# Attention stage of a hybrid decoder trunk: all score tiles scaled right behind the softmax's join, one weight pair fewer by seven products, and a written order for the seventh head

## The chip, the cores and the metric

The kernel runs on one core of one Trainium2 chip, in float32. The metric is the device time of one launch in microseconds (us). In the texts PE is the TensorE engine (matmuls and transposes), DVE is VectorE, ACT is ScalarE, POOL is GpSimd and SP is the engine that issues most transfers.

## The reference, cut to what matters

The trunk has four residual layers: attention, a gated FFN, a Mamba-2 mixer, a second gated FFN, then a final norm. The change touches the attention layer alone. There are 512 tokens, 1024 features, 8 heads of 128 in each of 3 groups, and each group has its own queries, keys and values:

```python
for g in range(3):                        # dilations 1, 4, 16
    o_g, lse_g = dilated_window_attention(q[:, :, g], k[:, :, g], v[:, :, g], ...)
wts = softmax(stack(lses), axis=2)        # over the three groups
o = einsum("bsgh,bsghe->bshe", wts, stack(outs, axis=2))
x = x + o.reshape(bsz, s, 1024) @ w_o     # 8 heads side by side
```

The head's output is one softmax over the keys of all three groups: the kernel takes the maximum and the sum over two sets of score columns, joins them, and scales every probability by its share before it multiplies with the values.

## The kernel before

**Precision.** A float32 product is made of three matmuls: each operand is split in a high and a low part (`hi`, `lo`, `xh`, `xl`), and high x high, high x low and low x high are added in one PSUM bank (`mm3`, all on L136). A weight unit of 128x1024 is loaded by SP into a `raw` tile, ACT casts the high part (`hi`, L127) and DVE subtracts (`lo`, L128).

**Query and key of one group of one head.** Plainly that is two units (`ready` loads, `qk_products` multiplies, `qk_read` reads): 24 matmuls of 128x512 each, then DVE multiplies by the cosines (L465) and shuffles (L468), and POOL multiplies by the sines and adds (L469, L470). For the pairs in `QK_PAIRS` query and key are made together by seven block products instead of eight (class `Pair`): 84 matmuls of 128x256 (seven `block`s), against 48 of 128x512. For it DVE makes sums of weight blocks (L317 to L321) and four splits (L331), and puts the results together (`query`: L525, L527; `key`: L532, L533, L534), then turns them (L541, L547, with POOL on L542 and L548). L534 is the last reader of the fourth product's bank, which comes from the `aux` banks.

**One head's attention** is the generator `attend(h)`, cut by `yield`s into stages: `scores(0)`, `scores(2)` (four score tiles, L648 to L650; DVE masks and takes maxima, ACT takes exponentials), `spread`, `join` (L676 to L684), `weigh(i)` (DVE scales score tile i by its share, two instructions each on L691), `by_key(i)` (PE transposes the tile, L698, and ACT copies it into a tile `pt`, L700), `values(i)` (PE, L706 and L711, into the banks `po` and `pg`). For heads 0 to 5 `attend_and_project(h)` weaves it with the products for head h+1. There PE, DVE and ACT follow the order in which the code is written (`WRITTEN`); SP and POOL are ordered by the framework's scheduler. PE's end of such a head reads: products of group 2 (the transposes of tiles 0 and 1 inside the second of them), values(0), by_key(2), by_key(3), values(1), 24 products of the next head's group 0 values (`v0_step`), values(2), values(3), and then scores(0) of the next head.

**Ahead of head 0** the pairs (0,1) and (0,2) are read by sevens, then the second half of group 0 plainly, then `v0_step(0)`. **Head 3** carries `late_values`, sixteen half steps of value weights, after its own work. **Heads 0 to 5** store their output; behind head 5 `fetch_heads` reads all six back and splits each in high and low (L753 on ACT, L754 on DVE), for the output projection `wo` that begins in head 7. In heads 6 and 7 the stages are woven by `together` and `weave`, and the scheduler orders PE, DVE and ACT as well, but for their last stage.

Of the kernel before, what the change touches and what calls it, by code (L numbers as in the profile page):

```python
# [9 lines left out]
F32 = mybir.dt.float32  # L10
# [4 lines left out]
P = 128  # L15
S = 512
# [4 lines left out]
NH = 8  # L21
NG = 3
DIL = 4
# [6 lines left out]
EPS = 1e-5  # L30
NEG = -1e30
FF_PARTS = ((0, 8), (8, 8), (16, 6))
QK_PAIRS = ((0, 1), (0, 2), (1, 1), (2, 1), (3, 1), (4, 1), (5, 1), (6, 1))
STORED = 6


# [17 lines left out]
def trunk(ctx: ExitStack, tc: tile.TileContext, A, out):  # L54
    nc = tc.nc
    V, SC, G, T = nc.vector, nc.scalar, nc.gpsimd, nc.tensor
    dma = nc.sync.dma_start

    cp = ctx.enter_context(tc.tile_pool(name="cp", bufs=1))
    wr = ctx.enter_context(tc.tile_pool(name="wr", bufs=4))  # L60
# [390 lines left out]
    def ready(h, g, c):  # L451
        u = A["wqk"][h * 7 + 2 * g + c]
        loaded[name_of(h, g, c)] = load_unit(u, name_of(h, g, c))

    def ready_v0(h):
        loaded[f"v0{h}"] = load_unit(A["wqk"][h * 7 + 6], f"v0{h}")

    def qk_products(h, g, c, cut=None):
        return project(A["wqk"][h * 7 + 2 * g + c], name_of(h, g, c), cut=cut)

    def qk_read(h, g, c, p):
        n = name_of(h, g, c)
        t = t2(n, "qk", 10, s3)
        at, of = (in_blocks, by_residue) if g == 0 else ((lambda ap: ap),) * 2
        V.tensor_tensor(at(t), of(p), of(cr), op=ALU.mult)  # L465
        rot = t2("rot" + n, "rot", 2, s3)
        R = slice(0, ROPE)
        V.stream_shuffle(rot[R, :], p[R, :], SWAP)  # L468
        G.tensor_tensor(rot[R, :], rot[R, :], sr[R, :], op=ALU.mult)  # L469
        G.tensor_tensor(at(t)[R], at(t)[R], of(rot)[R], op=ALU.add)  # L470
        qk[h, g, c] = t
# [86 lines left out]
    def v0_turn(h):  # L558
        t = v0[h]
        pv = aux_bank("pv")  # L560
        for j in range(4):
            T.transpose(pv[:, j * P : (j + 1) * P], t[:, j * P : (j + 1) * P], ident)
        v0[h] = t2(f"v0{h}", "v0", 2, s3)
        SC.copy(v0[h], pv)

    def qk_steps(h):
        return [
            lambda cut=None, g=g, c=c: qk_step(h, g, c, cut) for g in range(NG) for c in range(2)
        ] + [lambda: v0_step(h)]

    E = mybir.EngineType
    WRITTEN = {E.PE, E.DVE, E.Activation}

    with tc.manual_schedule(engines=WRITTEN):
        load2(1)
        V.tensor_tensor(cr, cr, rbc, op=ALU.mult)
        second[0]()
        combine(1)
        load2(2)
        V.tensor_tensor(sr[0:ROPE, :], sr[0:ROPE, :], rbc[0:ROPE, :], op=ALU.mult)  # L580
        second[1]()
        combine(2)
        load2(3)
        second[2]()
        combine(3)
        ready(0, 0, 0)
        one = Pair(0, 1)
        second[3]()
        one.sums()
        one.split("ab")  # L590
        p = qk_products(0, 0, 0)
        qk_read(0, 0, 0, p)
        one.split("cd")
        two = Pair(0, 2)
        for i in range(3):
            one.block(i)
        one.query(0)
        two.sums()
        two.split("a")
        for i in range(3, 6):  # L600
            one.block(i)
        one.query(1)
        two.split("b")
        one.block(6)
        one.turn(0)
        one.key()
        two.split("cd")
        for i in range(3):
            two.block(i)
        two.query(0)  # L610
        ready(0, 0, 1)
        for i in range(3, 6):
            two.block(i)
        two.query(1)
        two.block(6)
        two.turn(0)
        two.key()
        ready_v0(0)
        p = qk_products(0, 0, 1)
        qk_read(0, 0, 1, p)  # L620
        ready(1, 0, 0)
        v0_step(0)
        ready(1, 0, 1)
# [4 lines left out]
    def attend(h):  # L628
# [58 lines left out]
        def weigh(i):  # L687
            k0 = P if i == 0 else 0
            pr = prs[i]
            for w, cs in enumerate((slice(k0, 256), slice(256, 512))):  # L690
                V.tensor_scalar(pr[:, cs], pr[:, cs], share[:, w, i : i + 1], None, op0=ALU.mult)  # L691
# [29 lines left out]
        yield  # L721
        share = join()
        yield
        weigh(0)
        weigh(1)
        yield
        by_key(0)
        by_key(1)
        yield
        weigh(2)  # L730
        weigh(3)
        yield
        po, pg = aux_bank(f"po{h}"), aux_bank(f"pg{h}")
        values(0)
# [6 lines left out]
        o = t2(f"o{h}", "o", 1, s3)  # L741
# [7 lines left out]
    store = tc.dram_tile([STORED * P, S], F32, name="store")  # L749

    def split_head(h, o):
        o_h, o_l = high_low(f"o{h}")
        SC.copy(o_h, o)  # L753
        V.tensor_tensor(o_l, o, o_h.bitcast(F32), op=ALU.subtract)  # L754
        oh.append(o_h)
        ol.append(o_l)

    def fetch_heads():

        for j in range(STORED // 2):  # L760
            raw = wr.tile([P, 1024], F32, tag="raw", name=f"raw_o{j}")
            for i in range(2):
                h = 2 * j + i
                o = raw[:, i * S : (i + 1) * S]
                dma(o, store[h * P : (h + 1) * P, :])
                split_head(h, o)

    def weave(core, shares, fill):

        cost = [getattr(f, "products", 24) for f in fill]
        done = 0
        for i in range(len(shares)):
            next(core, None)
            while done < len(fill) and sum(cost[:done]) * sum(shares) < sum(cost) * sum(shares[: i + 1]):
                fill[done]()
                done += 1
# [9 lines left out]

    def together(core):  # L790

        for n in (1, 1, 2, 2, 2, 1):
            for _ in range(n):
                next(core, None)
            yield

    def attend_and_project(h, after=()):

        core, m = attend(h), h + 1
        follow = lambda c: ready(m + 1, 0, c)  # L800
        with tc.manual_schedule(engines=WRITTEN):
            pair = Pair(m, 1)
            next(core)
            pair.sums((0,))
            v0_turn(h)
            pair.split("a")
            pair.sums((1,))
            p = qk_products(m, 0, 0)
            qk_read(m, 0, 0, p)
            pair.split("bc")  # L810
            ready(m, 2, 0)
            p = qk_products(m, 0, 1)
            qk_read(m, 0, 1, p)
            next(core)
            for i in range(3):
                pair.block(i)
            pair.query(0)
            pair.split("d")
            ready(m, 2, 1)
            for i in range(3, 5):  # L820
                pair.block(i)
            next(core)
            pair.block(5)
            pair.query(1)
            next(core)
            next(core)
            pair.block(6)
            pair.turn(0)
            pair.key()
            ready_v0(m)  # L830
            p = qk_products(m, 2, 0)
            qk_read(m, 2, 0, p)

            def cut():
                next(core)
                next(core)

            p = qk_products(m, 2, 1, cut=(5, cut))
            next(core)
            qk_read(m, 2, 1, p)  # L840
            for f in after[:2] or (lambda: follow(0), lambda: follow(1)):
                f()
            v0_step(m)
            next(core, None)
            for f in after[2:]:
                f()
            if after:
                follow(0)
                follow(1)

    def late_values():

        (l1, s1), (l2, s2) = v_steps(1, 1), v_steps(2, 1)
        loads = [lambda l=l, u=u: l(u) for l in (l1, l2) for u in range(4)]
        steps = s1 + s2
        out = loads[:2]
        for i, f in enumerate(steps):
            if i + 2 < len(loads):
                out.append(loads[i + 2])
            out.append(f)  # L860
        return out

    for h in range(NH):
        if h < NH - 2:
            attend_and_project(h, late_values() if h == 3 else ())
            if h == STORED - 1:
                fetch_heads()
            continue
        if h < NH - 1:
            fill = qk_steps(h + 1)  # L870
            fill.pop()
        else:
            fill = [lambda: (v0_step(h), v0_turn(h))] + [lambda m=m: wo_first(m) for m in range(3)]
        core = together(attend(h))
        if h == NH - 2:
            v0_turn(h)
        weave(core, [1] * (DIL + 1), fill if h == NH - 1 else fill[:-1])
        with tc.manual_schedule(engines={mybir.EngineType.PE}):
            next(core, None)
            if h == NH - 1:  # L880
                wo_first(3)
                wo_first(4)
        if h < NH - 1:
            fill[-1]()

    att.__exit__(None, None, None)
    lp = ctx.enter_context(tc.tile_pool(name="lp", bufs=1, reuse_waits="tile"))
# [5 lines left out]
    for m in range(KD):  # L893
        if m not in wo_held:
            wo_first(m)
        hi, lo, p = wo_held[m]
# [868 lines left out]
```

## Time and profile before

| | |
|---|---|
| median of three runs | 1651.85 us (1650.76 to 1653.82) |
| the profiled execution | 1652.85 us, of which the span from the first to the last instruction is 1651.1 us |
| busy share of the span | PE 98%, DVE 76%, ACT 44%, POOL 34% |
| start to scores(0) of head 0 | 0 to 91.33 us: PE busy 86.10, DVE 72.13 |
| heads 0 to 6, to scores(0) of head 7 | 91.33 to 485.47 us (394.14): PE busy 371.37, DVE 287.83, POOL 141.26; mean granted clock 0.96 |
| head 7 to the first product of the FFN | 485.47 to about 542 us (56.5): PE busy throughout, clock 1.00 |
| FFN, Mamba-2, FFN, final norm | 1109 us: PE busy 1102.70 |

A row of the timeline gives the start in us, the duration of one instruction (or of the run of equal ones), the engine, the line, the operation, output <- inputs, shapes, and in brackets the idle time just before with what ended it. Matmuls are pipelined: their durations overlap, so what one costs is the distance between starts. A row of the stretches gives the length, and for each engine the busy time with the count of instructions, then the TensorE clock that was granted as a share of full speed.

### The profile page before, as it was taken

The numbers are of one execution on the slowest core, as the hardware profiler recorded it, in microseconds if no ns is written. First come the engines' busy times: TensorE is split into PE (matmuls) and PEld (weight loads), VectorE is DVE, ScalarE is ACT, GpSimd is POOL, SyncE is SP. The second block draws the span as 40 slices with busy tenths as digits, with TensorE's granted clock in tenths as the row PEclk, the third lists the DMA queues.
The fourth block names the chain that finished last, engine by engine and source line by source line (L and its number), as shares of the span: only waits on it lengthen the run. The fifth ranks groups of instructions, "written<-read, shape, count | busy, mean of one in ns | idle before, by whom it ended". The sixth has DMA issues, their size and how long they took to land.

```text
span 1651.1 us, 23543 instructions
## 1 busy us (share of the span) xinstructions
PE 1616.7 (98%) x8900; PEld 1410.5 (85%) x8900; DVE 1258.4 (76%) x2094; ACT 723.8 (44%) x1137; POOL 567.7 (34%) x432
## 2 busy tenths in 40 slices
PE   9999999999899999999999999999999999999998
PEld 8888788888788888988988888888888888988987
DVE  7887878267865777867856899888888687877864
ACT  6423323233334454444434545544544454444443
POOL 0344344024341274554323222210223265365230
PEclk9999999999999999999999999999999999999999
DMA  6322122222323322332334333334333222342341
GB/s 217 96 90 91 59 74 83 96 77 84 121 91 111 118 90 77 108 122 77 104 101 131 114 117 119 100 125 138 112 100 97 95 86 68 92 152 66 92 138 51
DMA packets 61889, 168.45 MB, mean 102 GB/s; under 512 B 7184, under 2 KB 10640, under 8 KB 61776
## 3 DMA queue, kind: packets, MB, share of 16 engines
q1 hardware_dynamic: 61216, 166.42, 31.4%
q8 instruction: 70, 1.15, 0.3%
q10 hardware_dynamic: 560, 0.53, 0.1%
q14 instruction: 43, 0.35, 0.1%
HBM read 163.19 MB, written 3.74 MB: 101 GB/s over the span
## 4 chain that ended last, share of the span: by engine, by line
PE 71%; DVE 3%; issue 1%; ACT 0%; POOL 0%; POOLq 0%; DVEq 0%; ACTq 0%
PE u L136 28%; PE xs L136 5%; PE wso L136 5%; PE z L136 5%; PE b L136 3%; PE c L136 3%; PE wo L136 3%; PE wd L136 2%; PE wz L136 2%; PE qk L136 1%; PE py L1338 1%; PE pf L1346 1%; PE pst L1293 1%; PE v L136 1%; PE wd113r L136 1%
## 5 line engine op out<-in xcount | busy, mean ns | idle before, releaser
L136 PE MATMUL u<-xh,hi_u 128*128 128x512 f32 x704 | 269.8, 383 | 0.0
L136 PE MATMUL u<-xh,lo_u 128*128 128x512 f32 x704 | 269.5, 383 | 0.0
L136 PE MATMUL u<-xl,hi_u 128*128 128x512 f32 x704 | 267.3, 380 | 0.0
L128 DVE TENSOR_TENSOR lo_u<-raw_u,hi_u 128x1024 fp32r<-128x1024 f32 x88 | 123.8, 1416 | 38.9 <-ACT hi_u L127 38.9
L136 PEld LDWEIGHTS u<-xh,lo_u 128*128 128x128 f32 x704 | 131.7, 187 | 25.0
L136 PEld LDWEIGHTS u<-xl,hi_u 128*128 128x128 f32 x704 | 131.7, 187 | 24.4
L136 PEld LDWEIGHTS u<-xh,hi_u 128*128 128x128 f32 x704 | 131.7, 187 | 22.6 <-issue 0.4
L127 ACT CAST hi_u<-raw_u 128x1024 fp32r<-128x1024 f32 x88 | 91.8, 1047 | 107.4 <-PE u L136 62.6
L469 POOL TENSOR_TENSOR rotqk<-rotqk,sr 32x512 f32<-32x512 f32 x32 | 64.7, 2023 | 206.2 <-DVE rotqk L468 206.2
L907 DVE SCALAR_TENSOR_TENSOR au<-u,par,au 128x511 f32<-128x511 f32 (+1 forms) x152 | 113.4, 746 | 20.5 <-ACT au L905 18.1
L932 POOL TENSOR_TENSOR au<-au,au 128x512 f32<-128x512 f32 x43 | 58.1, 1351 | 170.7 <-DVE au L907 156.8
L920 DVE TENSOR_TENSOR u<-u,rbc 128x512 f32<-128x512 f32 x76 | 52.9, 696 | 66.0 <-PE u L136 65.7
L1283 POOL TENSOR_TENSOR xdd<-xdt,dec 128x384 f32<-128x384 f32 x16 | 18.0, 1140 | 241.1 <-DVE xdt L1282 241.1
L136 PE MATMUL qk<-xh,hi_qk 128*128 128x512 f32 x256 | 99.4, 388 | 0.4 <-ACT hi_qk L127 0.4
L136 PE MATMUL qk<-xh,lo_qk 128*128 128x512 f32 x256 | 98.3, 384 | 0.5 <-DVE lo_qk L128 0.5
L136 PE MATMUL qk<-xl,hi_qk 128*128 128x512 f32 x256 | 97.3, 380 | 0.0
L905 ACT ACTIVATE au<-u,par 128x512 f32<-128x512 f32 x76 | 59.3, 780 | 23.0 <-DVE u L920 21.4
L239 POOL TENSOR_TENSOR ssum<-ssum,sq 128x512 f32<-128x512 f32 x21 | 32.5, 1550 | 84.3 <-ACT sq L238 83.9
L1083 POOL TENSOR_TENSOR xr<-xr,sums 128x512 f32<-128x512 f32 x16 | 33.1, 2069 | 82.1 <-DVE sums L1081 82.1
L660 ACT ACTIVATE pr<-pr,neg 128x256 f32<-128x256 f32 (+1 forms) x64 | 31.1, 487 | 68.2 <-DVE neg L658 67.6
L136 PEld LDWEIGHTS qk<-xh,lo_qk 128*128 128x128 f32 x256 | 47.9, 187 | 9.9 <-DVE lo_qk L128 1.0
L1392 POOL TENSOR_TENSOR lm<-lm,cb 128x512 f32<-128x512 f32 x32 | 47.4, 1506 | 25.5 <-ACT lm L1325 25.5
(3418 smaller groups left out, 4881.6 us busy)
## 6 DMA issues: line engine op xcount, KB each, us to landing
raw_u<-in_wup SPq DMA_DIRECT2D x88, 512.0 KB, 3.4
raw_qk<-in_wqk SPq DMA_DIRECT2D x32, 512.0 KB, 3.5
raw_xs<-in_win SPq DMA_DIRECT2D x16, 512.0 KB, 3.2
raw_z<-in_win SPq DMA_DIRECT2D x16, 512.0 KB, 3.4
lm<-rows SPq DMA_DIRECT2D x32, 256.0 KB, 5.0
raw_wso<-in_wso SPq DMA_DIRECT2D x16, 512.0 KB, 3.4
raw_v<-in_wv SPq DMA_DIRECT2D x12, 512.0 KB, 4.4
raw_wd<-in_wdn SPq DMA_DIRECT2D x16, 384.0 KB, 3.4
```

The costliest lines, as they stand in the source:

```text
L127: SC.copy(hi[:, s], raw[:, s])
L128: low.tensor_tensor(lo[:, s], raw[:, s], hi.bitcast(F32)[:, s], op=ALU.subtract)
L136: T.matmul(in_turns(dst), w, in_turns(x), start=first, stop=last, skip_group_check=skip)
L239: add.tensor_tensor(ssum, ssum, sq, op=ALU.add)
L469: G.tensor_tensor(rot[R, :], rot[R, :], sr[R, :], op=ALU.mult)
L660: SC.activation(pr[:, cs], pr[:, cs], AF.Exp, bias=neg[:, w, i : i + 1], scale=scale, accum_out=own[:, w, 1, i : i + 1],)
L905: latest["tap"] = SC.activation(dst, src, AF.Identity, bias=col(c_b), scale=col(c_w + taps - 1))
L907: V.scalar_tensor_tensor(dst[:, j:], src[:, : S - j], col(c_w + taps - 1 - j), dst[:, j:], op0=ALU.mult, op1=ALU.add,)
L920: V.tensor_tensor(dst, p, rbc, op=ALU.mult)
L932: by.tensor_tensor(ab[1], ab[0], ab[1], op=ALU.mult)
L1083: G.tensor_tensor(low3, low3, v.unsqueeze(1).to_broadcast([P, 2, 256]), op=ALU.add)
L1392: G.tensor_tensor(t, t, cb, op=ALU.mult)
```

## The change

It has four parts.

1. `QK_PAIRS` no longer has (0, 2): group 2 of head 0 is read plainly, and its four products and reads stand where the second pair's blocks stood.
2. In `attend`, the four `weigh` calls stand together right behind `join`; `by_key(0)`, `by_key(1)` follow, and values(0), by_key(2), by_key(3), values(1) are the next stage. In `attend_and_project` the split of the value unit (`ready_v0(m)`) moves ahead of the pair's turn and key.
3. The first two units of head 5 are split among head 3's late value loads instead of behind them.
4. Head 6 gets a function of its own, `attend_and_fetch`, with PE, DVE and ACT in written order; `fetch_heads` is called in three parts there and no longer at head 5's end.

```diff
-QK_PAIRS = ((0, 1), (0, 2), (1, 1), (2, 1), (3, 1), (4, 1), (5, 1), (6, 1))
+QK_PAIRS = ((0, 1), (1, 1), (2, 1), (3, 1), (4, 1), (5, 1), (6, 1))
...
-        two = Pair(0, 2)
+        ready(0, 2, 0)
...
+        ready(0, 2, 1)
...
         one.key()
-        two.split("cd")
...
+        p = qk_products(0, 2, 0)
         ready(0, 0, 1)
...
+        qk_read(0, 2, 0, p)
+        p = qk_products(0, 2, 1)
         ready_v0(0)
+        qk_read(0, 2, 1, p)
         p = qk_products(0, 0, 1)
...
         share = join()
         yield
-        weigh(0)
-        weigh(1)
+        for i in range(4):
+            weigh(i)
         yield
         by_key(0)
         by_key(1)
-        yield
-        weigh(2)
-        weigh(3)
         yield
         po, pg = aux_bank(f"po{h}"), aux_bank(f"pg{h}")
         values(0)
...
             pair.block(6)
+            ready_v0(m)
             pair.turn(0)
             pair.key()
-            ready_v0(m)
...
-            p = qk_products(m, 2, 1, cut=(5, cut))
+            p = qk_products(m, 2, 1, cut=(5, lambda: next(core)))
...
-            if after:
-                follow(0)
-                follow(1)
...
         loads = [lambda l=l, u=u: l(u) for l in (l1, l2) for u in range(4)]
+        loads += [lambda c=c: ready(5, 0, c) for c in range(2)]
...
+    def attend_and_fetch(h):
+        core, m = attend(h), h + 1
...
+            next(core)
+            v0_turn(h)
+            ready(m, 1, 0)
+            products(0, 0)
+            read(0, 0)
+            fetch_heads(0)
+            products(0, 1)
+            ready(m, 1, 1)
+            read(0, 1)
+            next(core)
+            products(1, 0)
+            ready(m, 2, 0)
+            next(core)
+            products(1, 1)
+            next(core)
+            next(core)
+            read(1, 0)
+            ready(m, 2, 1)
+            read(1, 1)
+            products(2, 0, cut=(5, lambda: next(core)))
+            next(core)
+            fetch_heads(1)
+            read(2, 0)
+            products(2, 1)
+            fetch_heads(2)
+            read(2, 1)
+            next(core, None)
```

The first place is DVE behind head 0's join. `pr` is a score tile, `join` holds the shares, the `qk` tiles with `keptqk` are the pair's key, `lo_v` is the low half of the next head's value unit. Before:

```order
L684 TENSOR_TENSOR join<-join 128x8
L691 TENSOR_SCALAR pr<-pr,join 128x128
L691 TENSOR_SCALAR pr<-pr,join 128x256 x3
L547 TENSOR_TENSOR qk_1108<-qk_1108,cr 128x512
L532 TENSOR_TENSOR qk_1109<-keptqk_1107,qk11r_1105 128x256
L533 TENSOR_TENSOR qk_1109<-qk_1109,keptqk_1107 128x256
L534 TENSOR_TENSOR qk_1109<-qk_1109,qk11r_1106 128x256
L541 STREAM_SHUFFLE rotqk_1248<-qk_1109 32x512
L547 TENSOR_TENSOR qk_1109<-qk_1109,cr 128x512
L128 TENSOR_TENSOR lo_v_1255<-raw_v_1253,hi_v_1254 128x1024
L465 TENSOR_TENSOR qk_1284<-qk_1259,cr 128x512
L691 TENSOR_SCALAR pr<-pr,join 128x256 x4
```

Now (the lines of the changed kernel are numbered anew: L683 is the scaling, L676 the join's last):

```order
L676 TENSOR_TENSOR join<-join 128x8
L683 TENSOR_SCALAR pr<-pr,join 128x128
L683 TENSOR_SCALAR pr<-pr,join 128x256 x7
L128 TENSOR_TENSOR lo_v_1186<-raw_v_1184,hi_v_1185 128x1024
L547 TENSOR_TENSOR qk_1045<-qk_1045,cr 128x512
L532 TENSOR_TENSOR qk_1046<-keptqk_1044,qk11r_1042 128x256
L533 TENSOR_TENSOR qk_1046<-qk_1046,keptqk_1044 128x256
L534 TENSOR_TENSOR qk_1046<-qk_1046,qk11r_1043 128x256
L541 STREAM_SHUFFLE rotqk_1195<-qk_1046 32x512
L547 TENSOR_TENSOR qk_1046<-qk_1046,cr 128x512
L465 TENSOR_TENSOR qk_1225<-qk_1200,cr 128x512
```

The last four scalings went from behind the key and the value unit's split to the join; that split went ahead of the turn and the key. PE's rows at this place are the same in both.

The second place is DVE ahead of head 0, from the first pair's last sums to group 0's second read. Before, behind the first pair's key (`qk_769` and `qk_770` are the second pair's query and key):

```order
L331 TENSOR_TENSOR loc_qk_757<-rawc_qk_629,hic_qk_756 128x1024
L331 TENSOR_TENSOR lod_qk_761<-q_qk_630,hid_qk_760 128x512
L525 TENSOR_TENSOR qk_769<-keptqk_768,qk02r_766 128x256
L128 TENSOR_TENSOR lo_qk_812<-raw_qk_810,hi_qk_811 128x1024
L527 TENSOR_TENSOR qk_769<-qk_769,qk02r_765 128x256
L541 STREAM_SHUFFLE rotqk_854<-qk_769 32x512
L547 TENSOR_TENSOR qk_769<-qk_769,cr 128x512
L532 TENSOR_TENSOR qk_770<-keptqk_768,qk02r_766 128x256
```

Now:

```order
L128 TENSOR_TENSOR lo_qk_775<-raw_qk_773,hi_qk_774 128x1024
L465 TENSOR_TENSOR qk_779<-qk_748,cr 128x512
L468 STREAM_SHUFFLE rotqk_781<-qk_748 32x512
L128 TENSOR_TENSOR lo_v_812<-raw_v_810,hi_v_811 128x1024
L465 TENSOR_TENSOR qk_816<-qk_785,cr 128x512
```

The weight sums, the four splits and the putting together of the second pair are gone; two units' splits stand earlier, among the first pair's rows, and two reads have come.

The third place is ACT around the end of head 5, where `o0h` to `o5h` are the high parts of the stored outputs. Before:

```order
L753 CAST o0h<-raw_o_3947 128x512
L753 CAST o1h<-raw_o_3947 128x512
L679 ACTIVATE join<-join 128x16
L127 CAST hi_v_3788<-raw_v_3787 128x1024
L753 CAST o2h<-raw_o_3958 128x512
L753 CAST o3h<-raw_o_3958 128x512
L753 CAST o4h<-raw_o_3969 128x512
L700 COPY pt<-pp 128x384
L700 COPY pt<-pp 128x512 x3
```

Now:

```order
L671 ACTIVATE join<-join 128x16
L127 CAST hi_v_3719<-raw_v_3718 128x1024
L692 COPY pt<-pp 128x384
L692 COPY pt<-pp 128x512 x3
```

The five casts that stood ahead of head 5's `pt` copies moved into head 6: two behind its first exponentials, four behind its own `pt` copies. From the first unit of the output projection on, PE, DVE and ACT have the same instructions in the same order in both kernels.

More of the change, by code (lines that the diff above doesn't have):

```diff
@@ L597, in trunk @@
         one.query(0)
-        two.sums()
-        two.split("a")
         for i in range(3, 6):
@@ L602, in trunk @@
         one.query(1)
-        two.split("b")
+        ready(0, 2, 1)
         one.block(6)
@@ L606, in trunk @@
         one.key()
-        two.split("cd")
-        for i in range(3):
-            two.block(i)
-        two.query(0)
+        p = qk_products(0, 2, 0)
         ready(0, 0, 1)
[L612 to L617, printed above, removed]
+        qk_read(0, 2, 0, p)
+        p = qk_products(0, 2, 1)
         ready_v0(0)
+        qk_read(0, 2, 1, p)
         p = qk_products(0, 0, 1)
@@ L756, in split_head, with fetch_heads @@
         ol.append(o_l)
[L758 to L766, printed above, removed]
+    def fetch_heads(j):
+        raw = wr.tile([P, 1024], F32, tag="raw", name=f"raw_o{j}")
+        for i in range(2):
+            h = 2 * j + i
+            o = raw[:, i * S : (i + 1) * S]
+            dma(o, store[h * P : (h + 1) * P, :])
+            split_head(h, o)
     def weave(core, shares, fill):
@@ L790, in together @@
     def together(core):
-        for n in (1, 1, 2, 2, 2, 1):
+        for n in (1, 1, 2, 2, 1, 1):
             for _ in range(n):
@@ L827, in attend_and_project @@
             pair.block(6)
+            ready_v0(m)
             pair.turn(0)
             pair.key()
-            ready_v0(m)
             p = qk_products(m, 2, 0)
             qk_read(m, 2, 0, p)
-            def cut():
-                next(core)
-                next(core)
-            p = qk_products(m, 2, 1, cut=(5, cut))
+            p = qk_products(m, 2, 1, cut=(5, lambda: next(core)))
             next(core)
@@ L861, in late_values, with products, read @@
         return out
+    def attend_and_fetch(h):
+        core, m = attend(h), h + 1
+        tiles = {}
+        def products(g, c, cut=None):
+            tiles[g, c] = qk_products(m, g, c, cut=cut)
+        def read(g, c):
+            qk_read(m, g, c, tiles[g, c])
+        with tc.manual_schedule(engines=WRITTEN):
+            next(core)
[25 more added lines that the diff above has]
+            next(core, None)
     for h in range(NH):
@@ L865, in trunk @@
             attend_and_project(h, late_values() if h == 3 else ())
[L866 to L871, printed above, removed]
+        elif h < NH - 1:
+            attend_and_fetch(h)
         else:
             fill = [lambda: (v0_step(h), v0_turn(h))] + [lambda m=m: wo_first(m) for m in range(3)]
[L874 to L880, printed above, removed]
+            core = together(attend(h))
+            weave(core, [1] * (DIL + 1), fill)
+            with tc.manual_schedule(engines={mybir.EngineType.PE}):
+                next(core, None)
                 wo_first(3)
                 wo_first(4)
-        if h < NH - 1:
-            fill[-1]()
     att.__exit__(None, None, None)
```

## The prediction

> **What bounds the kernel now.** I read the page first, then PE's waits, then PE's timeline around them. From the page:
>
> ```profile
> span 1651.1 us, 23543 instructions
> PE 1616.7 (98%) x8900; PEld 1410.5 (85%) x8900; DVE 1258.4 (76%) x2094; ACT 723.8 (44%) x1137; POOL 567.7 (34%) x432
> ```
>
> PE is the bound, and only 34.4 us of the span are without a matmul. The waits of PE from 0 to 600 us (total, times, longest) say where most of them lie:
>
> ```profile
> PE pp L698 <- DVE pr L691: 19.7, 20, 1.7
> PE qk02r L136 <- DVE loc_qk L331: 2.3, 1, 2.3
> PE po L706 <- ACT pt L700: 2.1, 1, 2.1
> PE qk02r L136 <- DVE qk L532: 1.1, 1, 1.1
> PE v L136 <- DVE lo_v L128: 0.8, 1, 0.8
> PE qk L136 <- DVE lo_qk L128: 0.5, 1, 0.5
> PE qk L136 <- ACT hi_qk L127: 0.4, 1, 0.4
> ```
>
> The first row is the transposes of score tiles that wait for their scaling. This is head 0 on PE:
>
> ```profile
> 126.80 0.38 PE L706 MATMUL po<-pt,v 128*128 128x128 f32 x2
> 129.01 0.41 PE L698 MATMUL pp<-ident,pr 128*128 128x128 f32 x2 [1.38 <-DVE pr L691]
> 130.24 0.44 PE L698 MATMUL pp<-ident,pr 128*128 128x128 f32 x2 [0.82 <-DVE pr L691]
> 131.57 0.90 PE L698 MATMUL pp<-ident,pr 128*128 128x128 f32 x4 [0.90 <-DVE pr L691]
> 139.97 0.60 PE L706 MATMUL po<-pt,v 128*128 128x128 f32 x4
> 141.75 0.39 PE L648 MATMUL sc<-qk,qk 128*128 128x128 f32 x2
> ```
>
> From values(0) to values(2) 13.17 us pass, of which the three waits are 3.10. They cost more than that. In the stretches (length; busy PE, PEld, DVE, ACT, POOL; clock) the clock falls behind them:
>
> ```profile
> 133.00:135.00 2.00, 2.00 (x9) 1.81 (x9) 0.95 (x2) 1.99 (x3) 1.81 (x2) 0.50 0.00 0
> 126.80:139.97 13.17, 10.07 (x47) 8.35 (x46) 9.83 (x13) 3.06 (x4) 7.68 (x5) 0.87 0.26 73
> 374.54:388.69 14.15, 11.09 (x47) 9.08 (x46) 9.89 (x13) 3.06 (x4) 7.95 (x5) 0.76 0.25 75
> sum 68.38, PE 52.28 PEld 42.85 DVE 50.41 ACT 15.31 POOL 39.66; mean PE 10.46 PEld 8.57 DVE 10.08 ACT 3.06 POOL 7.93
> ```
>
> The last three rows are the same stretch in the first and the last of heads 0 to 4, and the sum over those five: 68.38 us. [...]
>
> Why the scaling is late is on DVE in head 0:
>
> ```profile
> 119.70 1.08 DVE L691 TENSOR_SCALAR pr<-pr,join 128x128 f32<-128x128 f32 x4
> 121.75 1.36 DVE L533 TENSOR_TENSOR qk<-qk,keptqk 128x256 f32<-128x256 f32 x1
> 123.15 0.42 DVE L534 TENSOR_TENSOR qk<-qk,qk11r 128x256 f32<-128x256 f32 x1
> 125.07 2.31 DVE L128 TENSOR_TENSOR lo_v<-raw_v,hi_v 128x1024 fp32r<-128x1024 f32 x1
> 128.53 3.25 DVE L691 TENSOR_SCALAR pr<-pr,join 128x256 f32<-128x256 f32 x4
> ```
>
> The second four scalings start only at 128.53, behind the key, the value split and a read, and take 3.25 us where the first four took 1.08. In the meantime POOL was rotating:
>
> ```profile
> 121.56 1.27 POOL L548 TENSOR_TENSOR qk<-qk,rotqk 32x512 f32<-32x512 f32 x1 [3.08 <-DVE qk L547]
> 124.50:136.60 12.10, 9.00 (x44) 7.46 (x43) 11.05 (x14) 4.09 (x6) 9.90 (x6) 0.86 0.10 25
> 301.27 1.23 DVE L128 TENSOR_TENSOR lo_v<-raw_v,hi_v 128x1024 fp32r<-128x1024 f32 x1 [0.47 <-ACT hi_v L127]
> ```
>
> L533 (0.42 for its like, L534) ended with POOL's L548; the split of 2.31 us takes 1.23 elsewhere, in the last row. DVE and POOL delay each other by whole instructions. [...]
>
> **The change part by part.**
>
> *Heads 0 to 4.* The last four scalings move to 120.8, ahead of everything that delayed them, and at a time at which POOL has nothing to do until L547, which now stands behind them. They end near 121.9 (another 1.1 us, as the first four), so by_key(2) and by_key(3) find them 5 us early. PE's order at the place stays. Unstalled, the piece from values(0) to values(2) is: six passes of values(0), eight transposes and eight passes of values(1), 22 x 0.111 = 2.44 (the 16 passes of values(2) and values(3) take 139.97 to 141.75), and 24 products, 5.28 (the plain group's stretch below, 79.59 to 84.87): 7.7; I take 7.8. Five heads: 68.38 - 5 x 7.8 = 29.4 us.
>
> What is late next: the key. Behind 121.9 now come the value split (1.23 to 2.31), L547, L532, L533, L534 (0.6 + 0.45 + 0.45 to 1.36 + 0.42): L534 ends at 125.1 to 126.9, where it ended at 123.57. It frees the bank that values(0) takes at 126.80, so this costs nothing to 0.1. Then the shuffle, and POOL's six instructions, which were 9.90 us busy in 12.10 (the stretch above), nearly back to back: they end at 125.1 or 126.9 plus 0.7 plus 9.90 = 135.7 to 137.5. PE, unstalled, reaches scores(0) of the next head, which reads the last rotation, at 126.80 + 7.8 + 1.78 (139.97 to 141.75) = 136.4. So a wait of 0 to 1.1 us stands there; I take 0.6 in four of the heads (head 3 has the late values in between), +2.4. A single wait of this size leaves the clock: the one of 0.8 (the row of v above) lies in a stretch with 1.00, the last row below.
>
> *Ahead of head 0.* The stretches are the second pair, the second half of group 0, and v0 to scores(0) of head 0:
>
> ```profile
> 64.52:79.59 15.07, 11.69 (x86) 11.30 (x85) 13.46 (x16) 4.84 (x8) 7.33 (x4) 0.89 0.44 139
> 79.59:84.87 5.28, 5.28 (x26) 4.49 (x25) 5.02 (x9) 0.25 (x1) 4.67 (x3) 1.00 0.01 3
> 84.87:91.33 6.46, 5.67 (x25) 4.41 (x24) 3.70 (x5) 0.00 (x0) 5.84 (x4) 1.00 0.32 81
> ```
>
> The pair takes 15.07 with two waits (1.1 and 2.3) and 0.89 of the clock, because DVE is busy 13.46 of it. Without waits seven products cost less than eight; with them, two plain units cost 2 x 5.28 = 10.56. DVE loses four sums, four splits and eight steps of query and key for two splits and two reads, so that the splits come in time; then v0's wait of 0.8 goes as well (5.28 for 6.46). From 64.52 to scores(0): 4 x 5.28 = 21.1 instead of 26.81, -5.7; I take -5.6, since POOL's last rotation ends about when PE arrives. Bounds: -4.9 with v0's wait kept, -5.7.
>
> *Head 4's start.* The two waits of 0.4 and 0.5 are for units whose split stood behind the late values; they are among them now: -0.9 (bounds 0, if ACT casts them as late as before, and -1.0).
>
> *Heads 5 and 6.* Here the read-back of the stored heads stood ahead of head 5's copies:
>
> ```profile
> 427.23 0.62 ACT L753 CAST o4h<-raw_o 128x512 fp32r<-128x512 f32 x1 [5.10 <-DMA raw_o<-store]
> 427.75 0.96 ACT L700 COPY pt<-pp 128x384 f32<-128x384 f32 x2
> 428.28 0.49 PE L706 MATMUL po<-pt,v 128*128 128x128 f32 x2 [2.10 <-ACT pt L700]
> 467.88 1.13 PE L698 MATMUL pp<-ident,pr 128*128 128x128 f32 x7 [1.03 <-DVE pr L691]
> 485.47 0.38 PE L648 MATMUL sc<-qk,qk 128*128 128x128 f32 x2
> PE pp L698 <- DVE pr L691: 3.6, 5, 1.0
> 423.21:441.38 18.17, 13.95 (x67) 11.35 (x66) 16.12 (x22) 5.50 (x8) 9.03 (x6) 0.81 0.23 72
> ```
>
> The cast of o4h waited for a transfer, the `pt` copies behind it, and values(0) for them. Waits between 423 and 486 us (the row before the last is for that window): 3.6 + 2.1 = 5.7. The clock of 0.81 over 18.17 us costs 0.19 x 18.17 = 3.5. All of it is 9.2. In head 6 the products are now written such that unit splits stand between exponentials and the spread; I leave 0.4 for that: -8.8, bounds -6.5 (two waits of 1 us at new places) and -9.2. The casts and subtractions themselves (12 of about 0.6) run on ACT and DVE beside PE, which has head 6's 144 products to do; if that cover were gone they would be 7 us. SP's loads move with them: the read-back is issued later, by three transfers of two heads, and its first use is in head 7.
>
> *Head 7 and the rest* are the same instructions, and PE had no wait from 485.47 to 542: a shift.
>
> Sum: -29.4 + 2.4 - 5.6 - 0.9 - 8.8 = -42.3. The profiled execution is 1652.85, 1.0 above the median of the runs shown: 1610.5 for it, and against the median 1609.5 us. Bounds: no wait behind the POOL chain and the full -9.2 give -45.3, 1606.5; a wait of 1.1 in all heads and the small values of the others (-29.4 + 5.5 - 4.9 + 0 - 6.5) -35.3, 1616.5.
>
> **The rivals.**
>
> *A. POOL's chain becomes the wait.* The 9.90 us start two or three later and must end before scores(0). If POOL and DVE delay each other in a worse order (L548 and L469 took up to 2.1 us against 1.27), the wait is 2 us in heads 0 to 5, and the half clock behind it costs another 1: 6 x 3 = 18 instead of 2.4, 1625. For it: POOL is the only engine whose work did not come earlier. Against it: no row shows POOL above 9.9 us for the six, and the scalings, which held it up, have gone.
>
> *B. Only the waits go.* If the half clock has another cause than these gaps (other short transposes, say), heads 0 to 4 win only the part of the 20 waits that is theirs: 19.7 - 3.6 = 16.1 instead of 29.4, and heads 5 and 6 5.7 instead of 8.8: 1609.5 + 13.3 + 3.1 = 1626. Against it: in the same places where no wait was (values(2) and scores(0) at 139.97) rows come at full pace.
>
> *C. Slower: the key behind eight scalings.* One mechanism, on DVE in heads 0 to 5: scalings and split run against POOL at the slow price throughout (3.25 for four), 6.5 + 2.31, then L547 and three of 1.36: L534 ends at 119.70 + 13.6 = 133.3 instead of 126.80, and values(0) waits 6.5 us for its bank, with 2.3 for the clock (13.17 - 7.8 - 3.10). In the six heads with such a pair that is 52.8 against the 44.7 gained: +8.1, 1660. It decides from a wait of 5.2 us on (6 x 7.5 = 45), L534 after 132. Against it: POOL has nothing to run while the scalings run, since L548 waits for L547.
>
> *D. It doesn't do what it says.* DVE may bind these stretches by its total: from 126.80 to 139.97 it is busy 9.83 of 13.17 us, more than the 7.8 I leave PE. Then each head would keep 9.8 instead of 7.8: 5 x 2 = 10 more, 1619.5. Against it: 3.25 of the 9.83 are the scalings, which move out of this stretch, and 6.6 are left.
>
> **How the numbers follow.** Forecast 0.69; A 0.14; B 0.07; D 0.06; C 0.02; the rest, 0.02, is a time that does not move because a wait I don't see takes all back. Predicted 1609.5 us. The range from 1604 (2.5 below the lower bound, since a stall that goes may bring back more clock than I counted) to 1622 takes in the forecast's bounds and D and a mild A; A in full and B are left out. What a measurement of this kernel can tell from no change is about 0.2%, 3.3 us. Faster by more than that: all but C and the rest, 0.96; within it 0.02; slower 0.02.
>
> **What would show it.** In the changed profile: no wait of transposes (`pp`) for `pr` in heads 0 to 6; values(0) to values(2) in 7.7 to 8.2 us with the clock at 1.00; a wait of scores(0) for POOL below 1.1 us; the eight scalings in 2 to 2.5 us; group 2 of head 0 in 10.6 us without waits; scores(0) of head 0 at about 85.8 and of head 7 at about 443; the span from there on as before, within 1 us. The forecast is wrong if the clock falls although the waits are gone (B), if PE waits for L534 (C), or if the rows of POOL run later than PE by 2 us (A).

## The result, and the profile after

The changed kernel takes 1610.14 us (median of 4 runs, 1609.94 to 1611.16), the kernel before 1652.21 beside it. The ratio is 0.9746, 95% interval 0.9730 to 0.9763. The profiled execution is 1610.11 us. The first rows of the changed kernel's page:

```profile
span 1608.0 us, 23435 instructions
PE 1598.8 (99%) x8864; PEld 1398.7 (87%) x8864; DVE 1230.4 (77%) x2083; ACT 720.1 (45%) x1132; POOL 570.6 (35%) x432
```

PE's time without a matmul went from 34.4 to 9.2 us, and its busy time fell by another 17.9. Most of that is products that had run at half clock: 16.9 us of it lie in heads 0 to 6, where the count of matmuls is the same within one (the rows below), and the mean granted clock of the run went from 0.989 to 0.999. PE's waits from 0 to 600 us, all of them:

```profile
PE sc L642 <- POOL qk L470: 1.5, 3, 1.0
PE warm L376 <- DVE mhalf L109: 1.1, 1, 1.1
```

No transpose waits for its scaling any more, and no `po` for a copy. The row of `warm` was there before the change too. The only new wait is that of the score products for POOL's rotation. In stretches of the changed kernel (length; busy PE, PEld, DVE, ACT, POOL with counts; clock): from the first pair's first block to scores(0) of head 0; values(0) to values(2) in heads 3 and 4; scores(0) of head 0 to that of head 7; from there to the first product of the FFN; and the attention from the first block on:

```profile
54.69:85.62 30.93, 30.93 (x182) 27.63 (x180) 20.18 (x30) 7.05 (x9) 22.32 (x12) 1.00 0.32 107
256.95:264.75 7.80, 7.80 (x48) 6.92 (x46) 7.05 (x10) 2.96 (x4) 7.48 (x5) 1.00 0.16 43
344.81:352.62 7.81, 7.81 (x48) 6.93 (x47) 7.08 (x10) 2.97 (x4) 7.43 (x5) 1.00 0.11 27
85.62:440.55 354.93, 354.49 (x2072) 316.11 (x2072) 266.51 (x636) 133.76 (x262) 139.54 (x81) 1.00 0.29 93
440.55:498.77 58.22, 57.19 (x291) 48.87 (x290) 38.99 (x83) 25.26 (x46) 15.52 (x9) 1.00 0.38 126
54.69:498.77 444.08, 442.61 (x2541) 392.62 (x2540) 325.68 (x748) 166.07 (x317) 177.38 (x101) 1.00 0.31 99
```

The same stretches of the kernel before, as far as they were not shown:

```profile
54.82:91.33 36.51, 32.33 (x217) 29.90 (x216) 31.44 (x41) 9.43 (x14) 21.61 (x12) 0.95 0.34 103
91.33:485.47 394.14, 371.37 (x2073) 325.31 (x2071) 287.83 (x640) 136.72 (x265) 141.26 (x82) 0.96 0.27 88
485.47:542.22 56.75, 56.75 (x291) 48.93 (x290) 34.11 (x78) 23.42 (x44) 11.50 (x7) 1.00 0.31 102
54.82:542.22 487.40, 460.45 (x2578) 404.14 (x2577) 353.38 (x759) 169.56 (x322) 174.37 (x101) 0.96 0.28 91
```

So -5.6 us ahead of head 0, -39.2 in heads 0 to 6, +1.5 in head 7: -43.3 from the first block to the FFN. The rest of the program is the same within 0.4 us. In heads 0 to 6 PE is now busy for 354.49 of 354.93 us, at full clock: of the old waits nothing is left.

DVE in head 0, after:

```profile
113.97 2.12 DVE L683 TENSOR_SCALAR pr<-pr,join 128x128 f32<-128x128 f32 x8
116.01 1.22 DVE L128 TENSOR_TENSOR lo_v<-raw_v,hi_v 128x1024 fp32r<-128x1024 f32 x1
118.19 1.36 DVE L533 TENSOR_TENSOR qk<-qk,keptqk 128x256 f32<-128x256 f32 x1
119.58 0.42 DVE L534 TENSOR_TENSOR qk<-qk,qk11r 128x256 f32<-128x256 f32 x1
```

Eight scalings take 2.12 us and the value split 1.22, where the last four scalings alone took 3.25 and the split 2.31. POOL in the same head: the instruction ahead of its chain, then the first, fourth, fifth and last of the chain's six:

```profile
118.00 1.26 POOL L548 TENSOR_TENSOR qk<-qk,rotqk 32x512 f32<-32x512 f32 x1 [5.26 <-DVE qk L547]
120.94 1.78 POOL L542 TENSOR_TENSOR rotqk<-rotqk,sr 32x512 f32<-32x512 f32 x1 [1.68 <-DVE rotqk L541]
125.41 2.15 POOL L470 TENSOR_TENSOR qk<-qk,rotqk 32x512 f32<-32x512 f32 x1
127.53 2.25 POOL L469 TENSOR_TENSOR rotqk<-rotqk,sr 32x512 f32<-32x512 f32 x1
129.86 1.26 POOL L470 TENSOR_TENSOR qk<-qk,rotqk 32x512 f32<-32x512 f32 x1
```

POOL stood idle for the 5.26 us ahead of 118.00, and the scalings (113.97 to 116.1) ran in that time. The chain ends at 131.12, and the product that reads it starts at 131.17 (0.05 after it): POOL is now just in time.

### The profile page after: what moved, and what is told of

Read it like the earlier page. It is cut to its first block, busy times and chain, and to the rows that moved or that the text cites. A ratio compares the mean times of both kernels' runs of the same rounds, so it can differ in the third digit from the quotient of the medians.

```text
span 1608.0 us, 23435 instructions
## 1 busy us (share of the span) xinstructions
PE 1598.8 (99%) x8864; PEld 1398.7 (87%) x8864; DVE 1230.4 (77%) x2083; ACT 720.1 (45%) x1132; POOL 570.6 (35%) x432
## 4 chain that ended last, share of the span: by engine, by line
PE 85%; DVE 4%; POOL 1%; issue 1%; ACT 0%; DVEq 0%; POOLq 0%; ACTq 0%
PE u L136 29%; PE qk L136 7%; PE xs L136 5%; PE wso L136 5%; PE z L136 5%; PE v L136 4%; PE b L136 3%; PE c L136 3%; PE wo L136 3%; PE wd L136 2%; PE wz L136 2%; PE py L1351 1%; PE pf L1359 1%; PE pst L1306 1%; PE qk41r L136 1%
## 5 line engine op out<-in xcount | busy, mean ns | idle before, releaser
L469 POOL TENSOR_TENSOR rotqk<-rotqk,sr 32x512 f32<-32x512 f32 x34 | 74.4, 2188 | 157.6 <-DVE rotqk L468 157.6
L136 PE MATMUL qk<-xh,hi_qk 128*128 128x512 f32 x272 | 105.5, 388 | 0.0
L136 PE MATMUL qk<-xh,lo_qk 128*128 128x512 f32 x272 | 104.2, 383 | 0.0
L136 PE MATMUL qk<-xl,hi_qk 128*128 128x512 f32 x272 | 103.4, 380 | 0.0
L136 PEld LDWEIGHTS qk<-xl,hi_qk 128*128 128x128 f32 x272 | 51.0, 187 | 8.8
```

Of the source, the lines that this page charges most:

```text
L136: T.matmul(in_turns(dst), w, in_turns(x), start=first, stop=last, skip_group_check=skip)
```

## The experiments

Nine kernels ran. To leave out how early the first loads land (the first block starts between 54.5 and 55.9 us), the third column is the distance in each profiled execution from the first pair's first block to the first product of the FFN; before it is 487.40, after 444.08.

| kernel | median, ratio to before (95%) | first block to FFN | PE's new or remaining waits there, us |
|---|---|---|---|
| changed | 1610.14, 0.9746 (0.9730 to 0.9763) | 444.08 | scores for POOL 1.5 |
| first part alone | 1648.24, 0.9978 (0.9969 to 0.9987) | 482.10 | scalings 19.5, pt 2.1, the two at head 4's start 0.9 |
| second part alone | 1621.20, 0.9813 (0.9800 to 0.9826) | 454.18 | scalings 2.4, POOL 2.1, L534 0.8, the three ahead of head 0, the two at head 4's start |
| third part undone | 1612.15, 0.9759 (0.9745 to 0.9774) | 445.37 | unit splits 0.9, POOL 1.3 |
| fourth part undone | 1615.28, 0.9778 (0.9765 to 0.9792) | 449.68 | POOL 2.6, scalings 1.5, L534 0.7 |
| split behind the key | 1610.46, 0.9748 (0.9731 to 0.9764) | 444.01 | POOL 1.1 |
| scalings behind the key | 1619.89, 0.9805 (0.9790 to 0.9820) | 452.69 | POOL 8.5, scalings 0.6 |
| one more POOL instruction a head | 1613.72, 0.9767 (0.9753 to 0.9782) | 447.91 | POOL 4.6 |
| before, without rotation | 1613.23, 0.9765 (0.9749 to 0.9781) | 448.85 | the three ahead of head 0, the two at head 4's start |
| reads first | 1609.78, 0.9744 (0.9730 to 0.9757) | 443.35 | POOL 0.8 |

**The first part alone.**

```diff
-QK_PAIRS = ((0, 1), (0, 2), (1, 1), ...
+QK_PAIRS = ((0, 1), (1, 1), ...
```

with the plain reads of the diff above in its place, and the rest as before.

> The kernel before with the first part alone: group 2 of head 0 read plainly. Theory (the seven-product pair is bound by DVE there): scores(0) of head 0 at 85.6 instead of 91.33 us, the rest shifted, -5.7 us in all, about 1646.5. Rival (DVE's time there is only pushed on into head 0, whose splits stand behind it): scores(0) earlier, but the gain is given back in head 0, 1650 to 1652.

Its stretches, from the first block to scores(0) of head 0, and heads 0 and 2 from values(0) to values(2):

```profile
55.25:86.18 30.93, 30.93 (x181) 27.63 (x180) 20.17 (x30) 7.00 (x9) 22.32 (x12) 1.00 0.34 104
121.73:135.95 14.22, 11.24 (x48) 9.27 (x46) 9.55 (x13) 3.06 (x4) 7.63 (x5) 0.76 0.24 74
224.87:236.63 11.76, 8.39 (x48) 6.90 (x47) 10.33 (x13) 3.06 (x4) 7.97 (x5) 1.00 0.16 47
```

36.51 became 30.93, to the hundredth what the full change has there: -5.6 as forecast, and DVE's work was not pushed on. By the timed runs the part is worth 3.8 us (2.1 to 5.1): between the theory's 5.7 and the rival's 0 to 2, and less than the trace's -5.30 from the block to the FFN. The other rows show one thing that blurs it. Head 0's stretch, with nearly the waits of before (1.24, 0.84 and 0.90 for 1.38, 0.82 and 0.90), took 14.22 instead of 13.17, at a clock of 0.76 instead of 0.87. Head 2, with waits of 1.65, 0.82 and 0.89, took only 11.76, with no half clock at all (the kernel before: 1.69, 0.83 and 0.90, 13.47 us, clock 0.87). What the half clock adds to the same waits differs between executions, and between heads of one.

**The second part alone.**

```diff
-        weigh(0)
-        weigh(1)
+        for i in range(4):
+            weigh(i)
...
+            ready_v0(m)
             pair.turn(0)
             pair.key()
-            ready_v0(m)
```

> The kernel before with the second part alone: four scalings behind the join, value split ahead of the key. Theory (the waits and the half clock behind them both go): heads 0 to 4 win 29.4 us less about 0.5 for POOL, heads 5 and 6 win 3 to 5, while the 2.1 us wait for the pt copies behind the read-back stays; -33, about 1619. Rival (only the waits go, the clock has another cause): 16 in heads 0 to 4 and 3 in the others, -19, about 1633.

It is -33.2 in the trace and 31 us by the medians: the theory's -33, not the rival's -19. Heads 0 to 6 run at a clock of 1.00 here: with most of the waits the half clock is gone too. About 1.4 us of it are luck that belongs to the stage ahead of head 0, where this kernel is the kernel before; the stretches behind the 2.3 us wait for `loc_qk`, first in the kernel before, then in this one:

```profile
74.00:76.00 2.00, 1.91 (x9) 1.92 (x10) 2.00 (x4) 0.00 (x0) 1.16 (x1) 0.50 0.50 135
```

```profile
74.00:76.00 2.00, 1.99 (x17) 1.99 (x18) 2.00 (x3) 0.53 (x2) 1.09 (x1) 1.00 0.48 137
```

The same wait (2.33 and 2.30), the same place, and once half the clock is withheld and once nothing. In the kernel without rotation (below), with the kernel before's code at this place and a wait of 2.33, half the clock was withheld again (this stretch starts 0.15 us ahead of the first product):

```profile
75.00:77.00 2.00, 1.85 (x8) 1.85 (x9) 2.00 (x3) 0.00 (x0) 1.22 (x1) 0.55 0.40 125
```

The theory had the 2.1 us wait for the `pt` copies stay in head 5, and it did not. The trace names L534 for 0.8 us there, and scores(0) waits 1.97 for POOL. The next run shows the same, with its rows.

**The fourth part undone**: `fetch_heads` as before at head 5's end, and head 6 by the scheduler.

```diff
-        elif h < NH - 1:
-            attend_and_fetch(h)
+            if h == STORED - 1:
+                fetch_heads()
```

> The changed kernel with the fourth part undone: read-back at head 5's end, head 6 by the scheduler. Theory (the 9 us of heads 5 and 6 are half scaling, half read-back): the 2.1 us wait for pt in head 5 returns with its half clock, 4 to 6 us more than the changed kernel, about 1615. Rival 1 (all of it was the read-back and head 6's order): 9 more, 1619. Rival 2 (all of it was the scaling): 1610.

The size came out (5.6 in the trace, 5.1 by the medians), but not the mechanism, and the size is a difference: from scores(0) of head 5 to that of head 7 this kernel takes 7.0 us more than the changed one (93.19 and 86.15), and in head 7, where it has no wait, 1.5 less (56.74 and 58.22). On PE at the end of head 5, at the next scores and in head 6, then on DVE in head 5:

```profile
391.05 0.46 PE L698 MATMUL po<-pt,v 128*128 128x128 f32 x2 [0.70 <-DVE qk L534]
403.31 0.60 PE L642 MATMUL sc<-qk,qk 128*128 128x128 f32 x2 [2.08 <-POOL qk L470]
429.82 1.15 PE L690 MATMUL pp<-ident,pr 128*128 128x128 f32 x7 [1.03 <-DVE pr L683]
```

```profile
387.77 1.74 DVE L743 TENSOR_TENSOR o2l<-raw_o,o2h 128x512 fp32r<-128x512 f32 x1
389.44 0.68 DVE L743 TENSOR_TENSOR o3l<-raw_o,o3h 128x512 fp32r<-128x512 f32 x1
390.04 0.41 DVE L533 TENSOR_TENSOR qk<-qk,keptqk 128x256 f32<-128x256 f32 x1
```

The splits of the stored heads (o2l, o3l) sit between L532 and L533 on DVE, and the key, L534 and POOL's chain are late by the 2.2 us from 387.8 to 390.0. In the kernel before, o2l stood there too, but four scalings and the value split came behind the key: there L534 ended 1.65 us behind the first transposes (424.86 and 423.21), here 3.54 (390.91 and 387.37). The cost of the read-back in head 5 is then on DVE and POOL. The copies of `pt` come at nearly the same moment as L534 (their row starts at 390.14), so they hold PE no longer than the key does. The wait for the scaling in head 6 (1.03 and 0.48) is what it was before. Behind the single wait of 2.08 half the clock was withheld here; behind the 1.97 at the same place in the second part alone, nothing (the first 2 us behind each, this kernel first):

```profile
403.31:405.31 2.00, 2.00 (x8) 1.82 (x9) 2.00 (x2) 1.96 (x2) 0.00 (x0) 0.56 0.62 238
```

```profile
409.00:411.00 2.00, 2.00 (x14) 1.92 (x15) 1.82 (x2) 1.88 (x3) 0.00 (x0) 1.00 0.65 244
```

**The third part undone**: the first units of head 5 behind the late values.

> The changed kernel with the third part undone: head 5's first two units split behind the late values again. Theory: the waits of 0.4 and 0.5 at the head's start return, 1.0 more, 1611. Rival (the units come in time anyway once the scalings are early): no wait, 1610.

The waits of 0.40 and 0.54 are back at head 4's start, and the stretch is 1.3 us longer (2.0 by the medians), where 1.0 was expected: the theory's mechanism.

**Place or collision?** Two runs take one of them each. In the first the last four scalings stand behind the key but ahead of the value split, where POOL rotates:

```diff
-            ready_v0(m)
             pair.turn(0)
             pair.key()
+            next(core)
+            ready_v0(m)
```

Here `next(core)` runs weigh(2) and weigh(3), which are a stage of their own again.

> The changed kernel with the last four scalings behind the key and ahead of the value split: 3.4 us earlier than in the kernel before, but still in the time in which POOL rotates. Theory (what decides is the place in DVE's queue): the scalings still take about 3.2 us, but PE waits at most 0.7 per head, 1610 to 1616. Rival (what decides is that they run against POOL): the transposes wait as before, 1.0 and 0.8 and 0.9 in each of six heads with the half clock, 1630 to 1640.

Neither time came. DVE's last four scalings, the third of POOL's six instructions, and PE at the next scores:

```profile
120.06 3.25 DVE L683 TENSOR_SCALAR pr<-pr,join 128x256 f32<-128x256 f32 x4
```

```profile
125.78 2.20 POOL L469 TENSOR_TENSOR rotqk<-rotqk,sr 32x512 f32<-32x512 f32 x1 [3.16 <-DVE rotqk L468]
```

```profile
133.82 0.49 PE L642 MATMUL sc<-qk,qk 128*128 128x128 f32 x2 [1.62 <-POOL qk L470]
```

The scalings took 3.25 us as in the kernel before, and the transposes hardly waited (0.6 in all): the place decides that wait, as the theory had it. But the time it lost did not vanish. DVE's reads of group 2 came later by it, POOL stood idle for 3.16 us, and the scores waited 1.4 to 1.6 us in five heads, 8.5 in all (with 0.8 in head 7). It costs 8.6 us in the trace and 9.8 by the medians. This is the wait of the prediction's rival A, without the half clock that A put behind it: with one wait of up to 1.6 us a head, the mean clock of the run was 0.999.

In the second, the kernel before lacks POOL's two instructions on each query and key tile of heads 1 to 7 (the sine part of the rotation is left out of the computation):

```diff
+        if h == 0:
             G.tensor_tensor(rot[R, :], rot[R, :], sr[R, :], op=ALU.mult)
             G.tensor_tensor(at(t)[R], at(t)[R], of(rot)[R], op=ALU.add)
```

and the same in the class `Pair`.

> The kernel before, with the sine part of the rotation (POOL's two instructions for each query and key tile) left out in heads 1 to 7, so that POOL is idle there; DVE's order is as before, with the last four scalings behind the key, the value split and a read. Theory (place and collision each cost, and either one taken away is enough): without POOL the split, the key's middle sum and the scalings shrink by 1.1, 0.9 and 2.1 us, the scalings end near 127.7 where PE first needs them at 127.5, the transposes wait 0.5 us per head at most, and the time falls by 27 to 33, to about 1622. Rival (the place alone decides): the scalings are still behind the queue, PE waits about 1 us and more per head with the half clock, the time falls by less than 15, above 1637.

DVE's order is that of the kernel before, and now:

```profile
121.15 0.42 DVE L534 TENSOR_TENSOR qk<-qk,keptqk 128x256 f32<-128x256 f32 x1
123.45 1.22 DVE L128 TENSOR_TENSOR lo_v<-raw_v,hi_v 128x1024 fp32r<-128x1024 f32 x1
125.83 1.11 DVE L694 TENSOR_SCALAR pr<-pr,join 128x256 f32<-128x256 f32 x4
```

(L534 is the key's middle sum here, L533 before.) 1.36, 2.31 and 3.25 us became 0.42, 1.22 and 1.11, and no transpose waits. The stretch from the first block to the FFN is 38.6 us shorter, which is all of the 29.4 and 9.2 that the prediction counted for heads 0 to 6. The theory's direction held, but I had left heads 5 and 6 out of the sum. So the waits of these heads hung on DVE being delayed by POOL. In heads 0 to 4 each of two things was enough: to take the collision away, or to let the scalings start earlier. The read-back came earlier too: the cast of o4h came 4.0 us behind the first transposes before (427.23 against 423.21 us) and 1.7 here (396.53 against 394.80).

**The split behind the key** (`ready_v0(m)` back behind `pair.key()`, scalings as in the change).

> The changed kernel with the next head's value split behind the key again (scalings still behind the join). Theory (POOL's chain is what is late next; it starts earlier by the split's 1.2 us, but the split then stands ahead of the reads of group 2 and runs against POOL): the end of the chain moves by less than 1 us, 1609 to 1611. Rival 1 (the split's place was needed): the split of 2.3 us holds the reads, POOL ends 1 to 2 us later in heads 0, 1, 2, 4 and 5, 1615 to 1620. Rival 2 (the place cost time): all POOL waits go, 1609.5.

444.01 against 444.08: the place of the split doesn't matter as long as the scalings stand at the join, as the theory had it.

**One more POOL instruction**, a multiplication by one of the key's rotation in heads 0 to 5.

```diff
             pair.key()
+            r = pair.rot[1][0:ROPE, :]
+            G.tensor_tensor(r, r, ones[0:ROPE, 0:1].to_broadcast([ROPE, 512]), op=ALU.mult)
```

> The changed kernel with one more POOL instruction in each of heads 0 to 5, a multiplication of the key's rotation by one (32x512, 1.3 to 2.2 us like its neighbours). Theory (POOL's chain ends just when PE comes, with 0 to 0.4 us to spare): PE waits 1 to 2 us at the group 2 scores in four or five heads, 5 to 9 us more than the changed kernel, 1615 to 1619. Rival (there is slack of 2 us): no change, 1610.

+3.8 in the trace, +3.6 by the medians. All five scores that directly follow such a chain wait, 0.31 to 1.11 us. The chain has little slack, as the theory had it, but the sum was smaller than the 5 to 9 us expected: the instruction took 1.03 us in each head and not 1.3 to 2.2, and it adds 0.1 to 1.1 us of wait in a head (head 1 had 0.21 already, head 4 0.23) and not 1 to 2.

**Reads first.** In the changed kernel o4l and o5l stand on DVE ahead of head 6's last read, and head 7 waits 1.0 us for POOL. Here the reads go first:

```diff
             next(core)
-            fetch_heads(1)
             read(2, 0)
+            fetch_heads(1)
             products(2, 1)
-            fetch_heads(2)
             read(2, 1)
+            fetch_heads(2)
```

> The changed kernel with the last two reads of head 6 ahead of the read-back's second and third part. In the changed kernel DVE splits stored heads ahead of those reads, and PE waits 1.0 us at the group 2 scores of head 7 for POOL's rotation. Theory (that queue place costs it): the wait goes, and 1.0 to 1.5 us with it, about 1608.7. Rival (a unit split of the output projection that the scheduler puts there holds the read anyway): the wait stays, 1610.

Both in part: the wait falls from 1.03 to 0.36, the stretch by 0.7 us, and o2l, o3l and a split of the output projection's third unit still stand ahead of the last read. By the medians (1609.78 and 1610.14) the two kernels can't be told apart; the trace is the only evidence for 0.7 us.

## Why the prediction was right, point by point

1609.5 us were forecast and 1610.14 measured, and the span fell by 43.1 where the sum said 42.3. The terms:

| term | forecast | measured |
|---|---|---|
| heads 0 to 4, values(0) to values(2) | -29.4 (7.8 each) | about -29.5 (7.72 to 7.81 each) |
| wait for POOL's chain at the next scores | +2.4 | +0.4 (0.21 and 0.23 in heads 1 and 4) |
| ahead of head 0 | -5.6 | -5.6 |
| head 4's start | -0.9 | -1.3 (third part undone) |
| heads 5 and 6 | -8.8 | about -8.8: the 39.2 of heads 0 to 6 less 29.5 and 1.3, plus 0.4 |
| head 7 | 0 | +1.5 |

Two terms were wrong, by 2.0 and 1.5 us with opposite signs, and that they nearly cancel is luck. **POOL's chain**: the work was right (it ends at 131.12, the forecast's 135.7 to 137.5 is 130.1 to 131.9 in the changed kernel's time, which is 5.6 us earlier here), but I had scores(0) wait at its first product. The product that reads group 2 is in the third row of the scores (L642, behind L640 and L641), 0.49 us later in head 0 (130.68 and 131.17), and that is most of the 0.6 I charged a head.

**Head 7** was called "a shift" with the same instructions. They are the same in number (291 matmuls), but neither do their inputs come at the same time nor is PE's order the same. On DVE, the stored heads' splits, moved into head 6, stand ahead of the last read, and so the rotation comes late. Two rows of the changed kernel, the split of o5l and the read:

```profile
440.58 1.76 DVE L743 TENSOR_TENSOR o5l<-raw_o,o5h 128x512 fp32r<-128x512 f32 x1
443.40 0.67 DVE L465 TENSOR_TENSOR qk<-qk,cr 128x512 f32<-128x512 f32 x1
```

I had counted what the moved splits cover ("beside PE") and not who is queued behind them on DVE. And PE's order in head 7, which the framework's scheduler sets there, is not the same in both kernels, although the change section says so of everything from the output projection's first unit on. The first product of the output projection and the group 2 score, before and after:

```profile
491.91 0.38 PE L136 MATMUL wo<-o0h,hi_wo 128*128 128x512 f32 x1
493.89 0.60 PE L650 MATMUL sc<-qk,qk 128*128 128x128 f32 x4
```

```profile
447.00 0.38 PE L136 MATMUL wo<-o0h,hi_wo 128*128 128x512 f32 x1
448.40 0.71 PE L642 MATMUL sc<-qk,qk 128*128 128x128 f32 x4 [1.03 <-POOL qk L470]
```

Before, nine products of the projection stand ahead of the score (1.98 us); now one does. The score came 8.42 us behind scores(0) in the kernel before (493.89 and 485.47), and POOL's rotation is now there 7.8 us behind it (448.35 and 440.55). So with the old order the late rotation would have cost nothing, by this estimate; it took both. The wait is 1.03 of the 1.5 us. The other 0.4 is in PE's busy time (57.19 us for 56.75, with the same 291 matmuls), and its cause stays open. By this the sign "the span from there on as before, within 1 us" did not hold: 1165.6 us became 1167.5.

Two more steps came out right by a picture that was too simple. In heads 5 and 6 I blamed the cast that waited for a transfer. That reads the kernel before rightly (values(0) starts 0.53 us behind the start of the `pt` copies, 427.75 and 428.28), but it is not the whole cost: in the run with the fourth part undone DVE and POOL set the waits there, and without the rotation there are none. And the half clock was taken as a fixed price. In five heads together it comes out (the second part alone agrees), but for a single wait it was 0 or about 1.4 us in different executions, and for the three waits of a head the mean clock of the stretch was 0.76 in one head and 1.00 in another of the same execution (heads 0 and 2 of the first part alone). So the 5.6 us ahead of head 0 are what this execution of before had to lose; the timed runs give that part 3.8.

Of the rivals, A was the nearest: it did not come true in the change, since DVE's reads follow the key at once, and its wait (not its half clock) did when the last scalings stood some 5 us later. B is refuted by the second part alone (-33.2, not -19), C by L534, which ends at 120.0, 1.2 us ahead of values(0) at 121.17, D by the stretches, with DVE 7.05 busy of 7.80.

What followed the gaps was not the same in all runs: in the kernel before, three gaps of 0.6 to 1.7 us within five us (127.63 to 131.57 in head 0) were followed by half clock in each of heads 0 to 4 (0.76 to 0.87 over the stretch), and in the run of the first part alone in four of the five (head 2 kept 1.00); one gap of 1.4 to 1.6 us a head was followed by no half clock in the run with the scalings behind the key, where the mean clock of the run was 0.999.

## What to carry to other kernels

Short DVE instructions that PE waits for belong where POOL is idle, and ahead of work that only has to be done some time: four scalings cost 3.25 us beside POOL and 1.1 away from it, and the queue ahead of them had made them start at 128.53 instead of 120.78. When a wait goes, look at what the same move puts behind it: who is next on that engine, and which instruction of the consumer, not which stage, reads its result. A wait's cost is read from the clock in the stretch behind it, over several occurrences, not from the idle time alone.

## What the runs showed of the hardware

One wait of 2.3 us on PE was followed by half clock in two executions (0.50 and 0.55 over 2 us) and by a clock of 1.00 in a third, at the same place of the same code; at the scores of head 6 a wait of 2.08 us was followed by 0.56 over 2 us in one run and one of 1.97 by 1.00 in another. What decides between the two, no run here shows.

DVE's instructions took longer beside POOL's in some places, and POOL's beside DVE's. In head 0 of the kernel before, L533 began at 121.75 us, while POOL's L548 ran to 122.83, and took 1.36 us for the 0.42 of its like; the next L548 began at 126.37, while DVE's split ran to 127.38, and took 2.13 us for 1.27. The prediction puts it as if it were so wherever the two meet, and the trace doesn't show that: DVE's read L465 that began at 127.30, beside the same L548, took 0.68 us, as the next one did with POOL idle (0.67, from 131.71). In head 0 of the changed kernel, of POOL's seven 32x512 instructions from 118.00 to 131.12 us, those that began outside DVE's splits of the next weight units took 1.26 to 1.29 us (beside L547: 1.78), and the two that began while these splits ran took 2.15 and 2.25.
